# Second token tile routed first and its table rows requested earlier; one-hot rows laid out slot, token, key, with gate parts on ScalarE

## The chip, the cores and the metric

The kernel runs on one core of one Trainium2 chip. The metric is device microseconds of one execution. Three timed runs of the kernel before gave a median of 1670.44 us (1669.8 to 1672.08). The profiled execution took 1673.91 us; its span, from the first to the last instruction that the profile shows, is 1672.1 us.

## The reference

Two transformer blocks in sequence over 256 tokens of width 1024. The part that the change touches is the PEER layer at the end of the first block, which lets each token pick 128 of 16,384 small experts and sums their outputs:

```python
def peer(h, w_pq, sub_keys, u_emb, v_emb):
    q = (h @ w_pq).reshape(B, S, 8, 2, 128)
    sc = jnp.einsum("bshcd,hcnd->bshcn", q, sub_keys)      # 8 heads x 2 halves x 128 keys
    s_top, i_top = lax.top_k(sc, 16)
    cand = s_top[..., 0, :, None] + s_top[..., 1, None, :]
    cand_idx = i_top[..., 0, :, None] * 128 + i_top[..., 1, None, :]
    best, pos = lax.top_k(cand.reshape(B, S, 8, 256), 16)
    expert_idx = jnp.take_along_axis(cand_idx.reshape(B, S, 8, 256), pos, axis=-1)
    gate = jax.nn.softmax(best, axis=-1)
    # per token c, experts e: 8 heads x 16
    a = jax.nn.gelu(jnp.einsum("ced,cd->ce", u_emb[idx], hx), approximate=False)
    return jnp.einsum("ce,ced->cd", g * a, v_emb[idx])
```

`u_emb` and `v_emb` are tables of 16,384 rows of 1024 floats, 64 MB each.

## The kernel before, in words

Nearly all weights stream from HBM in blocks of 128x1024 floats (512 KB), issued by SyncE. A weight block of the ordinary layers is split into a high part (`whi`, made on ScalarE) and a low part (`wlo` = raw - high, made on VectorE, or on GpSimd for the blocks whose number is in `POOL`), and 24 matmuls use it (lines 145 to 147).

The PEER layer runs as follows (function `peer`). In this text a *u-block* is one block of 128 rows of the table u, a *v-block* the same of v.

1. Query stage. 16 weight blocks of `w_peer_q` (numbers 66 to 81) give the queries; `scores(h, c, qt)` makes the scores of head h, half c for the two token tiles `tt` = 0 and 1 (tokens 0 to 127 and 128 to 255). VectorE starts the routing from them: `unit(tt, h, ...)` finds the top 16 of both halves and of their sums, `select(tt, h0)` turns positions into expert numbers for four heads (`isel`, `jsel`), `gates()` makes the softmax (`ex`) and the expert number (`ei`). These are Python generators in the list `bg`; `pump(budget)` takes steps from its head until the budget, in microseconds of VectorE, is used. Where the instructions finally stand on an engine is set by a list scheduler with its own costs, not by the order of the calls alone.
2. u stage. 128 u-blocks (`ublock`), each 16 matmul instructions (line 976) and a Gelu into the array `G`. They serve tokens 0 to 159 densely (N = 160): all 16,384 experts are computed. The transfer of a block is asked for when one of ten buffers of the ring comes free.
3. One-hots. For four tokens at a time (40 groups), `onehots` makes Q and O, which compare `jT` and `iT` with the row of numbers `io`, and P and R, which are O times the high and the low part of the gate; `place` multiplies Q with P and R on TensorE (line 1009, 8 matmuls), and the result multiplies `G` (line 1015 on VectorE). So gates are spread over the dense grid of experts.
4. Rows. Tokens 160 to 255 are not computed densely: for them GpSimd asks for single table rows with an indirect DMA, 128 rows of 4 KB (512 KB) in one instruction (line 1555). There are two row groups, 192 to 255 and 160 to 191, together 96 row transfers of u, then 96 of v, into six buffers. A u transfer is followed by a dot product on VectorE (`dot`, line 1560), a v transfer by a multiply-add (`axpy`, line 1570). `some_rows(rate)` after each block takes steps of this sequence; the first row needs `idx`, which `indices` makes from `ei` by matmuls with `spread` (line 1547) and a copy on VectorE (line 1550).
5. v stage. 128 v-blocks, each 16 matmul instructions (line 1064), with the rest of the rows beside them, then the sum and the next layer.

Before the change `gates()` is called once for both token tiles, behind 46 u-blocks (`I0`); its transposes and index matmuls stand behind u-block 47 on TensorE.

Of the kernel before, what the change touches and what calls it, by code (L numbers as in the profile page):

```python
# [20 lines left out]
T = 256  # L21
# [38 lines left out]
POOL = range(4, 52)  # L60
# [11 lines left out]
QP = 1.3  # L72
UP = 2.0

NT = 4
RG = 0
# [9 lines left out]
class Kernel:  # L86
# [710 lines left out]
    def peer(self):  # L797
# [6 lines left out]
        iT = p2h.tile([128, T], F16, name="iT")  # L804
        jT = p2h.tile([128, T], F16, name="jT")
# [3 lines left out]
        gTl = p2h.tile([128, T], F16, name="gTl")  # L809
# [44 lines left out]
        def select(tt, h0):  # L854
# [40 lines left out]
        scs = {}  # L895

        def scores(h, c, qt):
            for tt in range(2):
# [24 lines left out]
        def gates():  # L923
            nc.vector.scalar_tensor_tensor(ei, isel, float(N_KEYS), jsel, op0=ALU.mult, op1=ALU.add)
            nc.vector.tensor_tensor(ex, best, best[:, :, :, 0:1].to_broadcast([128, 2, 8, 16]), op=ALU.subtract)
            nc.scalar.activation(ex, ex, AF.Exp)
            sm = p2t.tile([128, 2, 8], F32, name="sm", bufs=1)
            nc.vector.reduce_sum(sm, ex, axis=AX.X)
            nc.vector.reciprocal(sm, sm)
            nc.vector.tensor_mul(ex, ex, sm[:, :, :, None].to_broadcast([128, 2, 8, 16]))  # L930
# [11 lines left out]
            self.later(1, turn)  # L942

# [43 lines left out]
        def onehots(t0, oh, io):  # L987

            ts = slice(t0, t0 + NT)
            Q, O, P, R = (oh.tile([128, 128, NT], F16, name=n, bufs=2) for n in ("Q", "O", "P", "R"))  # L990
            col = lambda v: v[:, None, ts].to_broadcast([128, 128, NT])
            nc.vector.tensor_tensor(Q, io, col(jT), op=ALU.is_equal)
            nc.vector.tensor_tensor(O, io, col(iT), op=ALU.is_equal)
            nc.vector.tensor_mul(P, O, col(gTh))
            if t0 >= RG:
                for k in range(NT):
                    nc.scalar.activation(R[:, :, k], O[:, :, k], AF.Copy, scale=gT[:, t0 + k:t0 + k + 1])
            else:
                nc.vector.tensor_mul(R, O, col(gTl))
            return Q, (P, R)  # L1000

        def place(t0, n_i, oh):

            pt = self.pp.tile([128, 4, 128], F32, name="ax", bufs=4)
            Q, Ps = oh
# [16 lines left out]
        for i in range(I0):  # L1022
            ublock(i, 0)
            self.pump(UP if i < I0 - 2 else 1e9)
# [753 lines left out]
```

## Time and profile before

| | |
|---|---|
| timed runs, median (range) | 1670.44 us (1669.8 to 1672.08) |
| profiled execution / its span | 1673.91 us / 1672.1 us |
| TensorE busy over the span | 1594.9 us (95%) |
| VectorE / ScalarE / GpSimd busy | 68% / 38% / 21% |
| chain that ended last, over the span | PE 60%, DMA 19%, DVE 17% |
| u stage / v stage, from the timeline | 339.4 to 705.9 us / 705.9 to 1013.4 us |

In the profile PE is TensorE, PEld its weight loads, DVE VectorE, ACT ScalarE, POOL GpSimd, SP SyncE, which issues the block transfers. A group of instructions is named by its line, its engine, its operation and output<-input tiles; "idle before" is the time for which the engine stood still just ahead of them, with what ended it. In the tables of stretches, the DMA share is the mean busy share of the core's 16 DMA engines and GB/s what they moved.

### The profile page before, as it was taken

Reading aid. Unit: us, or ns where it says so; the run is one execution under the profiler, and the core shown is the slowest. Engines: PE = TensorE matmul, PEld = TensorE weight load, DVE = VectorE, ACT = ScalarE, POOL = GpSimd, SP = SyncE. Lnnn points to the kernel's source line nnn. Section 1 sums busy time; section 2 is a strip of 40 time slices with the busy share of each in tenths; the row PEclk is TensorE's granted clock in tenths of the full one; section 3 lists DMA queues with packets and bytes.
Section 4 is the critical chain, followed back from the end, with each engine's and each line's share of the span. In section 5 each row is a group of like instructions: output and inputs, shape, how many; then the busy total and the mean of one; then the engine's idle time right before and its main releaser. Section 6 shows DMA issues by size and latency. Waiting matters only on the chain.

```text
span 1672.1 us, 29794 instructions
## 1 busy us (share of the span) xinstructions
PE 1594.9 (95%) x11502; PEld 1504.6 (90%) x11502; DVE 1142.8 (68%) x2599; ACT 637.1 (38%) x1373; POOL 347.1 (21%) x288
## 2 busy tenths in 40 slices
PE   8989989998989899899999999999999999999998
PEld 7878979998989899899888999887999998799986
DVE  7989978898178899854544007866776557676654
ACT  4557545531233343200000005455544445555443
POOL 3734630000045454543332000100000020000000
PEclk9989989999999999899999999999999999999999
DMA  5522437576799999999999865732755677365563
GB/s 184 171 80 93 137 123 228 160 252 198 239 402 406 408 381 409 395 409 409 409 409 409 317 196 159 246 102 87 224 185 182 186 189 211 94 188 183 180 189 113
DMA packets 109388, 398.97 MB, mean 239 GB/s; under 512 B 12484, under 2 KB 12643, under 8 KB 108736
## 3 DMA queue, kind: packets, MB, share of 16 engines
q1 hardware_dynamic: 78336, 282.63, 50.0%
q0 software_dynamic: 30768, 114.39, 18.1%
q8 instruction: 90, 1.47, 0.4%
q14 instruction: 50, 0.41, 0.1%
q10 hardware_dynamic: 144, 0.07, 0.0%
HBM read 394.86 MB, written 6.11 MB: 240 GB/s over the span
## 4 chain that ended last, share of the span: by engine, by line
PE 60%; DMA 19%; DVE 17%; issue 3%; ACT 1%; POOL 1%; SPq 0%; DVEq 0%; POOLq 0%; ACTq 0%
PE mm L145 12%; PE mm L146 11%; PE mm L147 11%; PE ax L1064 9%; DMA row<-un,idx 8%; DMA raw<-vv 4%; DMA whi<-vv 4%; PE mm L976 3%; DVE junk L1560 2%; DVE ax L589 2%; PE mm L213 1%; DVE wlo L126 1%; PE mm L211 1%; PE mm L212 1%; PE ax L442 1%
## 5 line engine op out<-in xcount | busy, mean ns | idle before, releaser
L122 ACT ACTIVATE whi<-raw 128x1024 fp32r<-128x1024 f32 x275 | 290.3, 1058 | 620.1 <-DMA raw<-wst 310.0
L126 DVE TENSOR_TENSOR wlo<-raw,whi 128x1024 fp32r<-128x1024 f32 x227 | 277.3, 1223 | 187.8 <-ACT whi L122 184.3
L145 PE MATMUL mm<-xgh,whi 128*128 128x256 f32 x1064 | 304.3, 286 | 0.0
L147 PE MATMUL mm<-xgh,wlo 128*128 128x256 f32 x1064 | 301.8, 284 | 0.4 <-DVE wlo L126 0.4
L146 PE MATMUL mm<-xgl,whi 128*128 128x256 f32 x1064 | 301.4, 283 | 0.0
L145 PEld LDWEIGHTS mm<-xgh,whi 128*128 128x128 f32 x1064 | 201.9, 190 | 1.1 <-issue 0.8
L147 PEld LDWEIGHTS mm<-xgh,wlo 128*128 128x128 f32 x1064 | 201.9, 190 | 0.7 <-DVE wlo L126 0.6
L146 PEld LDWEIGHTS mm<-xgl,whi 128*128 128x128 f32 x1064 | 202.0, 190 | 0.1
L1570 DVE SCALAR_TENSOR_TENSOR acc<-row,w,acc 128x1024 f32<-128x1024 f32 x94 | 120.7, 1284 | 111.1 <-DMA row<-vv,idx 111.0
L1555 POOL DMA_INDIRECT row<-un,idx x96 | 105.5, 1099 | 277.6 <-DVE idx L1550 169.4
L1560 DVE CUSTOM_DVE_ANT_0 junk<-row,h 128x1024 f32<-128x1024 f32 x96 | 117.5, 1224 | 33.9 <-DMA row<-un,idx 32.4
L124 POOL TENSOR_TENSOR wlo<-raw,whi 128x1024 fp32r<-128x1024 f32 x48 | 115.1, 2403 | 107.8 <-ACT whi L122 105.0
L1064 PE MATMUL ax<-G,raw 128*128 128x160 f32 x832 | 125.6, 303 | 3.1 <-DMA raw<-vv 1.0
L1555 POOL DMA_INDIRECT row<-vv,idx x96 | 96.7, 1008 | 142.8 <-DVE acc L1570 123.5
L1064 PEld LDWEIGHTS ax<-G,raw 128*128 128x128 f32 x832 | 116.1, 191 | 8.1 <-DMA raw<-vv 7.7
L976 PE MATMUL mm<-hn,raw 128*128 128x160 f32 x816 | 121.6, 304 | 0.1
L976 PEld LDWEIGHTS mm<-hn,raw 128*128 128x128 f32 x816 | 116.5, 195 | 0.4 <-ACT G L984 0.3
L146 PE MATMUL mm<-hl,whi 128*128 128x256 f32 x368 | 106.8, 290 | 2.2 <-DVE hl L356 2.1
L976 PE MATMUL mm<-hn,wlo 128*128 128x160 f32 x608 | 95.3, 313 | 5.0 <-ACT G L979 5.0
L589 DVE SCALAR_TENSOR_TENSOR ax<-u,cw,ax 128x256 f32<-128x256 f32 x227 | 97.7, 481 | 0.7
L1064 PE MATMUL ax<-G,wlo 128*128 128x160 f32 x608 | 93.6, 306 | 2.2 <-DMA wlo<-vv 0.6
L976 PEld LDWEIGHTS mm<-hn,wlo 128*128 128x128 f32 x608 | 90.5, 201 | 5.2 <-ACT G L979 5.2
(435 smaller groups left out, 3358.2 us busy)
## 6 DMA issues: line engine op xcount, KB each, us to landing
raw<-wst SPq DMA_DIRECT2D x278, 512.0 KB, 3.7
raw<-vv SPq DMA_DIRECT2D x52, 512.0 KB, 15.1
raw<-ut SPq DMA_DIRECT2D x51, 512.0 KB, 6.6
whi<-ut SPq DMA_DIRECT2D x39, 512.0 KB, 6.6
wlo<-ut SPq DMA_DIRECT2D x38, 512.0 KB, 6.7
wlo<-vv SPq DMA_DIRECT2D x38, 512.0 KB, 14.9
whi<-vv SPq DMA_DIRECT2D x38, 512.0 KB, 15.5
tabr<-tabd POOLq DMA_DIRECT2D x1, 2048.0 KB, 8.3
```

Of the source, the lines that this page charges most:

```text
L122: nc.scalar.activation(hi, raw, AF.Copy)
L124: nc.gpsimd.tensor_sub(lo, raw, hi)
L126: self.pin = nc.vector.tensor_sub(lo, raw, hi)
L145: nc.tensor.matmul(pt, w[:, s], xs[0][:, k], start=first, stop=False)
L146: nc.tensor.matmul(pt, w[:, s], xs[1][:, k], start=False, stop=False)
L147: nc.tensor.matmul(pt, lo[:, s], xs[0][:, k], start=False, stop=last)
L589: nc.vector.scalar_tensor_tensor(y[:, c] if k == 30 else ps, u[:, c, k:k + T], cw[:, c, k:k + 1], ps, op0=ALU.mult, op1=ALU.add)
L976: nc.tensor.matmul(pt, raw[:, k * 128:(k + 1) * 128], hn[:, k, :N], start=(k == 0), stop=(k == C - 1))
L1064: nc.tensor.matmul(acc[d // 2][:, d % 2, :N], raw[:, d * 128:(d + 1) * 128], G(i), start=False, stop=False, skip_group_check=True)
L1555: self.k.nc.gpsimd.indirect_dma_start(t, None, table, bass.IndirectOffsetOnAxis(ap=self.idx[:, s:s + 1], axis=0))
L1560: self.k.nc.vector.tensor_tensor_reduce(junk, row, self.h, 1.0, 0.0, ALU.mult, ALU.add, self.a[:, s:s + 1])
L1570: self.k.nc.vector.scalar_tensor_tensor(self.acc, row, w, self.acc, op0=ALU.mult, op1=ALU.add)
```

## The change

Routing order: `scores` handles token tile 1 first and puts the routing of tile 1 ahead of tile 0 in `bg`; `gates(tt)` is one call for each tile, and the one of tile 1 also starts the row requests (`indices`). The 16 query blocks get their `wlo` on GpSimd, and the budgets are new (QP from 1.3 to 2.8; UP from 2.0 to 2.1 and, once the rows are asked for, 1.4). For tile 0 one of the three wide operations of `select` runs on GpSimd. The u-blocks run without a fixed I0 until `bg` is empty, with `some_rows(0.68)` after each once the rows are asked for, and `some_rows(0.8)` after each v-block; before, both rates were 197 steps over 206 blocks.

One-hots: Q and O become one tile QO (slot, token, key) from one VectorE instruction with three buffers; P and R are both made on ScalarE by 8 scaled copies of 128 elements, where R alone took 4.

```diff
-POOL = range(4, 52)
+POOL = (*range(4, 52), *range(66, 82))
-QP = 1.3
-UP = 2.0
+QP = 2.8
+UP = (2.1, 1.4)
+RU = 0.68
+RV = 0.8
...
-                nc.vector.tensor_mul(e4, e4, tops[:, tt, c, h0:h0 + nh, None, :].to_broadcast([128, nh, 16, 16]))
+                eng.tensor_tensor(e4, e4, tops[:, tt, c, h0:h0 + nh, None, :].to_broadcast([128, nh, 16, 16]), op=ALU.mult)
...
-            for tt in range(2):
+            for tt in (1, 0):
...
-                self.bg.append(turns(*(unit(tt, h, [scs[tt, h, i] for i in range(2)]) for tt in range(2))))
-                if h % 4 == 3:
-                    self.bg.extend([select(tt, h - 3) for tt in range(2)])
+                u0, u1 = (unit(tt, h, [scs[tt, h, i] for i in range(2)]) for tt in range(2))
+                firsts.append(u1)
+                self.bg.insert(next((k for k, u in enumerate(self.bg) if k and u not in firsts), len(self.bg)), u1)
+                self.bg.append(u0)
...
             def turn():
-                for n, src in enumerate((isel, jsel, ex)):
-                    pt = self.pp.tile([128, T], F32, name="ax", bufs=4)
-                    for tt in range(2):
-                        nc.tensor.transpose(pt[:, tt * 128:(tt + 1) * 128], src[:, tt].rearrange("p a b -> p (a b)"), self.ident)
-                    nc.scalar.activation((iT, jT, gT)[n], pt, AF.Copy, scale=(1.0, 1.0, G_SCALE)[n])
-                self.split(gT, gTh, gT)
-                nc.scalar.activation(gTl, gT, AF.Copy)
-                for g in rows:
-                    g.indices()
+                if tt == 1:
+                    for g in rows:
+                        g.indices()
+                    asked.append(tt)
+                pt = self.pp.tile([128, 3, 128], F32, name="ax", bufs=4)
+                for n, src in enumerate((jsel, isel, ex)):
+                    nc.tensor.transpose(pt[:, n], at(src).rearrange("p a b -> p (a b)"), self.ident)
+                nc.scalar.activation(jiT[:, :, ts], pt[:, :2], AF.Copy)
+                nc.scalar.activation(gT[:, ts], pt[:, 2], AF.Copy, scale=G_SCALE)
+                self.split(gT[:, ts], gTh[:, ts], gTl[:, ts])
             self.later(1, turn)
...
-            Q, O, P, R = (oh.tile([128, 128, NT], F16, name=n, bufs=2) for n in ("Q", "O", "P", "R"))
-            col = lambda v: v[:, None, ts].to_broadcast([128, 128, NT])
-            nc.vector.tensor_tensor(Q, io, col(jT), op=ALU.is_equal)
-            nc.vector.tensor_tensor(O, io, col(iT), op=ALU.is_equal)
-            nc.vector.tensor_mul(P, O, col(gTh))
...
+            QO = oh.tile([128, 2, NT, 128], F16, name="QO", bufs=3)
+            P, R = (oh.tile([128, NT, 128], F16, name=n, bufs=2) for n in ("P", "R"))
+            nc.vector.tensor_tensor(QO, io[:, None, None, :].to_broadcast([128, 2, NT, 128]),
+                                    jiT[:, :, ts, None].to_broadcast([128, 2, NT, 128]), op=ALU.is_equal)
+            for k in range(NT):
+                for dst, g in ((P, gT), (R, gTl)):
+                    nc.scalar.activation(dst[:, k], QO[:, 1, k], AF.Copy, scale=g[:, t0 + k:t0 + k + 1])
...
-        I0 = 46
-        for i in range(I0):
+        k = next((k for k, u in enumerate(self.bg) if k and u not in firsts), len(self.bg))
+        self.bg[k:k] = [select(1, 0, nc.vector), select(1, 4, nc.vector), gates(1)]
+        self.bg += [select(0, 0, nc.gpsimd), select(0, 4, nc.gpsimd), gates(0)]
+        done, i = 0, 0
+        while self.bg:
             ublock(i, 0)
-            self.pump(UP if i < I0 - 2 else 1e9)
-        gates()
-        done, i = 0, I0
+            self.pump(UP[len(asked)])
+            if asked:
+                some_rows(RU)
+            i += 1
```

Three places show how instructions move. The first is TensorE in the u stage before the change: the matmuls on `hn` are u-blocks (x8 is one block; the profile shows each of its matmuls as two instructions), and 47 blocks stand ahead of the transposes of `isel`, `jsel`, `ex` and the index matmuls on `spread`.

```order
L976 MATMUL mm<-hn,raw 128x160 x8
L976 MATMUL mm<-hn,whi 128x160 x8
L976 MATMUL mm<-hn,wlo 128x160 x8
L936 MATMUL ax<-ident,isel 128x128 x2
L936 MATMUL ax<-ident,jsel 128x128 x2
L936 MATMUL ax<-ident,ex 128x128 x2
L1547 MATMUL ax<-ei,spread_4060 128x128
L1547 MATMUL ax<-ex,spread_4060 128x128
```

After the change the index matmuls of tile 1 stand behind u-block 11; this is TensorE there.

```order
L987 MATMUL mm<-hn,raw 128x160 x16
L1560 MATMUL ax<-ei,spread_4209 128x128
L1560 MATMUL ax<-ex,spread_4209 128x128
L1560 MATMUL ax<-ei,spread_4219 128x128
L1560 MATMUL ax<-ex,spread_4219 128x128
L948 MATMUL ax<-ident,jsel 128x128
L948 MATMUL ax<-ident,isel 128x128
L948 MATMUL ax<-ident,ex 128x128
```

The transposes of tile 0 follow behind u-block 36, and the first one-hot product stands behind u-block 40 (before: behind block 49). The second place is VectorE just ahead of the first one-hots, before the change: no dot product (`junk<-row`) precedes the first Q.

```order
L1550 CAST idx_4064<-ax 32x32
L1551 COPY gate_4065<-ax 32x32
L1035 CAST io<-iota 128x512
L1067 MEMSET zeros 128x512
L992 TENSOR_TENSOR Q<-io,jT 128x512
L993 TENSOR_TENSOR O<-io,iT 128x512
L994 TENSOR_TENSOR P<-O,gTh 128x512
L1560 ISA junk,a_4056<-row,h_4052 128x1024
```

The same place after the change.

```order
L1573 ISA junk,a_4205<-row,h_4201 128x1024
L1573 ISA a_4205 128x1
L358 TENSOR_TENSOR gTl<-gT,gTh 128x128
L1049 CAST io<-iota 128x128
L1080 MEMSET zeros 128x512
L1003 TENSOR_TENSOR QO<-io,jiT 128x1024 x3
L1573 ISA junk,a_4205<-row,h_4201 128x1024
```

30 dot products stand ahead of the first QO, between it and the copies to `idx`; before the last QO of the 40 there are 140 row steps (96 dots, 44 multiply-adds), where before the change 100 stood ahead of the last Q (96 and 4). The third place is GpSimd. Before, its row transfers follow the `park` transfer, with nothing between them:

```order
L124 TENSOR_TENSOR wlo<-raw,whi 128x1024 x48
L811 DMA sk<-subk 128x2048
L802 DMA park<-x 128x2048
L1555 DMA row<-un,idx_4054 128x1024 x64
L1555 DMA row<-un,idx_4064 128x1024 x32
```

The same place after the change:

```order
L813 DMA sk<-subk 128x2048
L126 TENSOR_TENSOR wlo<-raw,whi 128x1024 x2
L804 DMA park<-x 128x2048
L126 TENSOR_TENSOR wlo<-raw,whi 128x1024 x14
L1568 DMA row<-un,idx_4203 128x1024 x11
L885 TENSOR_TENSOR eq<-eq,tops 128x1024
L1568 DMA row<-un,idx_4203 128x1024 x2
```

GpSimd has 16 more low parts ahead of the row transfers, and the four products of `select` for tile 0 stand among the first 18 of them, the first behind 11.

## Rows read from the trace of the kernel before

**Rows 1.** Stretches: us, busy (instructions) of PE, PEld, DVE, ACT, POOL; clock, DMA, GB/s.

```profile
276.00:339.00 63.00, 62.86 (x535) 62.51 (x533) 55.30 (x230) 32.97 (x70) 0.55 (x1) 1.00 0.60 195
339.00:390.00 51.00, 51.00 (x382) 50.90 (x382) 51.00 (x287) 13.53 (x31) 0.00 (x0) 1.00 0.73 237
390.00:396.00 6.00, 1.23 (x10) 0.98 (x8) 5.96 (x43) 1.84 (x3) 0.00 (x0) 0.81 0.56 190
...
480.00:520.00 40.00, 33.30 (x249) 32.55 (x248) 31.30 (x70) 14.07 (x58) 18.84 (x18) 1.00 1.03 407
...
456.00:706.00 250.00, 224.89 (x1611) 220.78 (x1610) 212.81 (x481) 91.34 (x368) 124.14 (x111) 0.96 1.01 397
706.00:925.00 219.00, 211.43 (x1438) 198.93 (x1437) 108.86 (x88) 0.00 (x0) 78.73 (x82) 0.99 1.03 409
```

**Rows 2.** Timeline of TensorE, u-blocks and index matmuls: start, length, line, tiles, count.

```profile
428.85 2.34 PE L976 MATMUL mm<-hn,raw 128*128 128x160 f32 x16
...
450.59 2.34 PE L976 MATMUL mm<-hn,raw 128*128 128x160 f32 x16
...
453.42 0.39 PE L1547 MATMUL ax<-ei,spread 128*128 128x128 f32 x2
```

**Rows 3.** Timeline of VectorE: routing from its start to the expert numbers.

```profile
294.16 2.85 DVE L891 SCALAR_TENSOR_TENSOR hn<-x,prm,rb 128x256 f32<-128x256 f32 x7
...
385.80 0.29 DVE L818 MAX8 tv<-sc 128x8 f32<-128x128 f32 x1
...
393.27 0.19 DVE L861 TENSOR_SCALAR q<-pos 128x64 uint32<-128x64 uint32 x1
...
411.77 0.43 DVE L924 SCALAR_TENSOR_TENSOR ei<-isel,jsel 128x256 f32<-128x256 f32 x1
```

**Rows 4.** Block transfers of table u issued by 456 us: ns, first to last start.

```profile
L966 SPq DMA_DIRECT2D raw<-ut x23: 327/328/328, 320.8 to 453.0; - x23
L966 SPq DMA_DIRECT2D whi<-ut x17: 327/328/423, 332.5 to 448.6; - x17
L966 SPq DMA_DIRECT2D wlo<-ut x17: 327/328/902, 333.0 to 450.8; - x17
```

**Rows 5.** DMA issues, 456 to 706 us: count, KB, median us to landing.

```profile
raw<-vv SPq DMA_DIRECT2D x4, 512.0 KB, 7.9
row<-un,idx POOLq DMA_INDIRECT x96, 11.1
wlo<-vv SPq DMA_DIRECT2D x3, 512.0 KB, 7.8
whi<-vv SPq DMA_DIRECT2D x3, 512.0 KB, 7.6
row<-vv,idx POOLq DMA_INDIRECT x15, 11.4
```

**Rows 6.** DMA issues, 706 to 925 us.

```profile
row<-vv,idx POOLq DMA_INDIRECT x81, 13.7
```

**Rows 7.** Chain that ended last, in order of time, through the v stage.

```profile
705.92 72.19 PE ax L1064 x512
778.13 20.67 DMA raw<-vv
...
923.13 75.52 PE ax L1064 x554
```

**Rows 8.** Groups by line, VectorE, 456 to 706 us: busy, mean ns, idle before.

```profile
L1560 DVE CUSTOM_DVE_ANT_0 junk<-row,h 128x1024 f32<-128x1024 f32 x96 | 117.5, 1224 | 33.9 <-DMA row<-un,idx 32.4 <-DVE O L993 0.5
L992 DVE TENSOR_TENSOR Q<-io,jT 128x512 f16<-128x512 f16 x40 | 16.8, 420 | 0.0
```

**Rows 9.** Groups by line and shape, VectorE, 339 to 412 us.

```profile
L879 DVE TENSOR_TENSOR eq<-f,iota 128x1024 f32<-128x1024 f32 x8 | 9.8, 1220 | 0.0
```

**Rows 10.** Groups by line, ScalarE, 456 to 706 us.

```profile
L997 ACT ACTIVATE R<-O,gT 128x128 f16<-128x128 f16 x160 | 63.0, 585 | 1.8 <-DVE O L993 1.8
```

**Rows 11.** Line 124, low parts on GpSimd: duration ns min/median/max, first to last.

```profile
L124 POOL TENSOR_TENSOR wlo<-raw,whi x48: 2337/2397/2607, 22.4 to 230.0; 128x1024 fp32r<-128x1024 f32 x48
```

More of the change, by code (lines that the diff above doesn't have):

```diff
@@ L803, in peer @@
         hn = p2h.tile([128, C, T], F32, name="hn")
-        iT = p2h.tile([128, T], F16, name="iT")
-        jT = p2h.tile([128, T], F16, name="jT")
+        jiT = p2h.tile([128, 2, T], F16, name="jiT")
         gT = p2h.tile([128, T], F32, name="gT")
         gTh = p2h.tile([128, T], F16, name="gTh")
-        gTl = p2h.tile([128, T], F16, name="gTl")
+        gTl = p2h.tile([128, T], F32, name="gTl")
         sk = p2q.tile([128, 16, 128], F32, name="sk")
@@ L852, in unit, with select @@
             yield from top16(best[:, tt, h], pos[:, tt, h], cd, w)
-        def select(tt, h0):
+        def select(tt, h0, eng):
             nh = 4
@@ L895, in peer @@
         scs = {}
+        firsts = []
         def scores(h, c, qt):
-            for tt in range(2):
+            for tt in (1, 0):
                 sp = self.pp.tile([128, 128], F32, name="ax", bufs=4)
@@ L921, in peer, with gates @@
         ex = p2t.tile([128, 2, 8, 16], F32, name="ex")
[L923 to L928, printed above, removed]
+        asked = []
+        def gates(tt):
+            at = lambda t: t[:, tt]
+            nc.vector.scalar_tensor_tensor(at(ei), at(isel), float(N_KEYS), at(jsel), op0=ALU.mult, op1=ALU.add)
+            nc.vector.tensor_tensor(at(ex), at(best), best[:, tt, :, 0:1].to_broadcast([128, 8, 16]), op=ALU.subtract)
+            nc.scalar.activation(at(ex), at(ex), AF.Exp)
+            sm = p2t.tile([128, 8], F32, name="sm", bufs=1)
+            nc.vector.reduce_sum(sm, at(ex), axis=AX.X)
@@ L942, in gates @@
             self.later(1, turn)
+            yield 1.5
         self.close("p2q")
@@ L989, in onehots @@
             ts = slice(t0, t0 + NT)
-            Q, O, P, R = (oh.tile([128, 128, NT], F16, name=n, bufs=2) for n in ("Q", "O", "P", "R"))
-            col = lambda v: v[:, None, ts].to_broadcast([128, 128, NT])
-            nc.vector.tensor_tensor(Q, io, col(jT), op=ALU.is_equal)
-            nc.vector.tensor_tensor(O, io, col(iT), op=ALU.is_equal)
-            nc.vector.tensor_mul(P, O, col(gTh))
[L995 to L1000, printed above, removed]
+            QO = oh.tile([128, 2, NT, 128], F16, name="QO", bufs=3)
[5 more added lines that the diff above has]
+                    nc.scalar.activation(dst[:, k], QO[:, 1, k], AF.Copy, scale=g[:, t0 + k:t0 + k + 1])
+            return QO, (P, R)
         def place(t0, n_i, oh):
             pt = self.pp.tile([128, 4, 128], F32, name="ax", bufs=4)
-            Q, Ps = oh
+            QO, Ps = oh
             for t in range(4):
@@ L1008, in place @@
                     k = (t0 + t) % NT
-                    nc.tensor.matmul(pt[:, t], Q[:, :, k], P[:, :, k], start=P is Ps[0], stop=P is Ps[-1])
+                    nc.tensor.matmul(pt[:, t], QO[:, 0, k], P[:, k], start=P is Ps[0], stop=P is Ps[-1])
             for k in range(2):
@@ L1033, in peer @@
         poh = self.open("poh", side="left")
-        io = poh.tile([128, 128, NT], F16, name="io")
-        nc.vector.tensor_copy(io, self.iota[:, :, None].to_broadcast([128, 128, NT]))
+        io = poh.tile([128, 128], F16, name="io")
+        nc.vector.tensor_copy(io, self.iota)
         i0 = i
         n_g = N // 4
-        rate = fetch_steps() / (254.0 - i0)
         for g in range(n_g):
@@ L1043, in peer @@
                 ublock(i, 4 * done)
-                some_rows(rate)
+                some_rows(RU)
                 i += 1
@@ L1049, in peer @@
             ublock(i, N)
-            some_rows(rate)
+            some_rows(RU)
             i += 1
@@ L1075, in peer @@
                 vmm(blk, d)
-            some_rows(rate)
+            some_rows(RV)
         self.close("pgb")
@@ L1088, in peer @@
                 vmm(blk, d)
-            some_rows(rate)
+            some_rows(RV)
         for _ in fetch:
@@ L1574, in add @@
         self.k.nc.tensor.matmul(o[:, self.t0:self.t0 + self.n], self.acc[:, c * 128:(c + 1) * 128], self.fold, start=False, stop=last, skip_group_check=True)
-def fetch_steps():
-    return 2 * sum(n for _, n in ROWS) + RB - 1
 def fetched(groups):
```

7 lines of the change are left out of this document (4 added, 3 removed).

## The prediction

> **What bounds the kernel now.** I read the table of stretches first, then the chain, then the timelines and DMA issues of the stretches that the change touches. In the stretches [rows 1] the reader is to see four states of the PEER layer. In the query stage (276 to 339 us) TensorE is full. From 339 to 390 us TensorE and VectorE are both full and the DMA engines move 237 GB/s: a u-block takes TensorE (450.59 - 428.85) / 10 = 2.174 us [rows 2], and 512 KB (0.524 MB) in that time is 241 GB/s. From 456 to 706 us, with the row transfers running, the DMA engines move 397 GB/s, and 409 from 706 to 925 us; TensorE has gaps there. So the DMA engines are the limit from the first row request until the rows are through, and TensorE before and after. Then the chain [rows 7]: TensorE runs unhindered from 705.92 to 778 us on blocks that were fetched ahead, then steps of some 20 us that end on v-blocks alternate with nothing else until 923 us, then TensorE alone, to the end of the stage at about 1013.4 us.
>
> Before 456 us some 409 - 241 = 168 GB/s lie idle. That is because the index matmuls stand behind u-block 47 and start only at 453.42 us [rows 2], though the expert numbers are finished at 411.77 + 0.43 = 412.2 us [rows 3].
>
> **When the first row is asked for after the change (T0).** On VectorE, from its start at about 293.4 us (294.16 less part of the low part ahead of it) to the copies to `idx`, the order shows the scaling of `hn` (8 x 0.4 = 3.3 us), 14 units (8 of tile 1, 6 of tile 0), two selects, gates for one tile and some set-up. Two units take 393.27 - 385.80 = 7.47 us, so 14 take 52.3. From 393.27 to 411.77 us VectorE does two selects and the gates of both tiles: 18.5 us, less about 0.7 for the smaller gates. Sum 3.3 + 52.3 + 17.8 + 2 for set-up and copies = 75.4, so 369 us. Before, the steps of both tiles alternated; now many wait for their predecessor, for which I add 0 to 8 us and take 4: T0 = 373 us. The scores are no limit: the last ones stand ahead of the u stage at 339 us, when half of this work is left. TensorE reaches the index matmuls behind block 11 at 339.4 + 11 x 2.174 = 363 us and waits little; `ei` is ready 3 units (11 us) ahead of the copies. The wait costs 0 to 5 us of TensorE, which it has to spare (below).
>
> **The u stage, by DMA transfers.** Count 512 KB transfers. By 456 us, 23 + 17 + 17 = 57 blocks were issued [rows 4]: the 47 that TensorE had done and the ring of ten. From 456 to 706 us 71 u-blocks, 4 + 3 + 3 = 10 v-blocks and 96 + 15 = 111 rows followed [rows 5]: 192 transfers in 250 us, 0.768 a us.
>
> At T0 after the change TensorE has done (373 - 339.4) / 2.174 = 15.5 blocks, with the ring 26 issued. At the end of the u stage 138 are issued as before. The rows by then are set by VectorE's order: TensorE can't finish the one-hot products before VectorE has made the last QO, and 140 row steps stand ahead of that, where 100 stood before. Before, 111 were issued when the stage ended, 11 more than the order asks; the same now gives 151. So 138 - 26 + 151 = 263 transfers, at 0.768 a us 342 us: the stage ends at 373 + 342 = 715 us, 9 us later than the 706 before, with 40 more rows fetched. If those 11 shrink to 6, it ends at 709; I take 713. Per us of T0, only (0.768 - 0.46) / 0.768 = 0.4 us is lost, since u-blocks flow meanwhile at 1 / 2.174 = 0.46.
>
> What must fit under it. TensorE: 128 x 2.174 = 278 us, 320 one-hot matmuls, and stalls: from 390 to 396 us [rows 1] it waited for ScalarE, which sat behind the Exp of the gates. Now there are two Exps; the second, behind the Gelu of block 24, waits for VectorE and may cost 7 to 10 us. With at most 0.14 us for each one-hot matmul, TensorE would be through at 339 + 278 + 45 + 15 = 677 us, 36 ahead. It will wait at block 40 (its 30 dots come ahead of the first QO: 50 blocks and some 36 rows, 60 transfers after T0, 78 us, 451 us), but this is the same DMA time again. VectorE: 212.81 us busy in the stage before [rows 1] for 107 row steps and 40 groups. From 451 us on it has 116 row steps (+9 x 1.22 = 11 us [rows 8]), 37 QO instead of 120 instructions of 0.42 us (-50), and 9 more blocks (+2). At 1.22 us for a QO it is 221 us of 263, 84% as before (85%). ScalarE: 8 copies a group at 0.585 us [rows 10] is 4.7 us of a group time of 7: hidden, and if not, a copy that is late holds the product of its group. GpSimd in the query stage: 2.40 us a low part [rows 11] against 24 x 63 / 535 = 2.83 us of TensorE a block [rows 1]: hidden; without that cover each of 16 would cost up to 2.4 us.
>
> The QO instruction itself isn't in the trace. Bounds: 0.42 us x 2 = 0.84 us for 1024 elements by the two-byte row for 512 [rows 8], 1.22 us by the four-byte row for 1024 [rows 9]. I take 1.22, the dearer, since one operand now stands still along the inner dimension. The Trainium skill ("VectorE: DVE Perf Modes", "What auto-detection actually checks") says that two results a cycle need every tensor 16-bit with step 1 or -1; the operand `jiT` has step 0, so that rule speaks against the change: three fast instructions become a slow one. By the rule the 37 QO take 45 us, without it 31; neither moves the sum, as the DMA engines end last by 40 us.
>
> **The v stage.** Before, 705.9 to 1013.4: 307.5 us with its tail. Its matmuls run at 75.52 / 554 = 0.1363 us when nothing is missing [rows 7], so the 1438 from 706 to 925 us [rows 1] need 196 of 219 us: 23 us lost to the DMA engines, all after the unhindered 72 us, so 23 / 147 = 0.16 us a us. The rows came at 81 in 203 us (706 to 909), 0.40 a us [rows 6]. After the change 192 - 151 = 41 to 46 are left, gone after 103 to 115 us; past the first 72 that is 31 to 43 us at 0.16, 5 to 7 us lost instead of 23. So the stage takes 307.5 - 17 = 290.5 us, bounds 284.5 (nothing lost) and 300.
>
> **Sum.** 713 + 290.5 = 1003.5 against 1013.4, so -10 us. Made against the profiled execution (1673.91 us, of which 1672.1 are span and the 1.8 around it stay) this gives 1664; that execution is 3.5 us over the median of the runs, which goes from 1670.44 to 1660. What lies ahead and behind is unchanged. The change buys little because the u stage is as full as before and only takes over rows that the v stage paid for.
>
> **Rivals.**
> *Better overlap* (bigger gain): with a third QO buffer and P off VectorE, the DMA engines run at the 409 GB/s of the next stretch, 0.78 transfers a us; T0 is 369 (24 blocks issued) and 146 rows come by the end: 138 - 24 + 146 = 260 transfers, 333 us, the u stage ends at 702, and the v stage loses nothing (284.5): 987, -27, 1643. For it: TensorE was idle for 250 - 224.89 = 25 us of this stage [rows 1]. Against: the DMA engines moved 397 GB/s through those gaps.
> *Rows hidden anyway* (no change): VectorE's interleaved routing delays the dots, and with them the freeing of six row buffers, so that T0 is 380 (0.4 x 7 = 3 us) and the rate until 451 us some 0.69 instead of 0.768 (71 x 0.08 = 5.5 transfers, 7 us). The gain of 10 is gone. For it: while the rows run, dots are spread between routing steps; against: six buffers hide some of that. Time 1670.
> *VectorE's queue as the bound* (slower): 30 dots stand ahead of the first QO and three a group after it, each waiting for its row in order, with QO, the products into `G` and so TensorE behind them. It decides once VectorE's busy share in the stage falls under 221 / (263 + 10) = 81%. In the first 40 us of full DMA load before, 480 to 520, it was 31.30 / 40 = 78% [rows 1]; at that share 221 us take 283, the stage ends at 451 + 283 = 734 and the v stage (289) at 1023: +9, 1680. For it: 32.4 us of waits of dots for rows before [rows 8]; against: three QO buffers.
>
> **Chances.** Forecast 0.53, better overlap 0.22, no change 0.13, slower 0.12. A difference under 0.2% (3.3 us) can't be told from none. The forecast's own spread is 1652 to 1668 (5 us from the count of rows, 4 from T0 and stalls each way); of the better case 1644 and up is taken in, of the slower one only what ends by 1671, so about 0.18 is left out. Faster 0.76, same 0.12, slower 0.12: the better case and nine tenths of the forecast are faster, and the unchanged case has its edges on both sides.
>
> **What would show it.** The first row request at 368 to 380 us; first one-hot product at 445 to 460 us; DMA engines full from about 375 us; end of the u stage within 705 to 722 us; rows through at 810 to 835 us instead of 909, and TensorE alone at 2.18 us a v-block afterwards; QO at about 1.2 us. The prediction is wrong if the DMA engines stay under 390 GB/s between 451 and 700 us (then VectorE bounds), if TensorE loses time in the query stage, or if far fewer than 140 rows are in by the end of the u stage.

## The result, and the profile after

The changed kernel takes 1699.63 us (median of 4 runs, 1696.7 to 1700.08) against 1670.12 us of the kernel before in the same session (1669.34 to 1672.08): 1.0171 times as long, interval 1.0154 to 1.0189. Slower by 1.7%, clear of the noise, where 1660 us was forecast. The profiled execution took 1699.78 us, with a span of 1698.0.

The stretches after, with the columns of [rows 1]: the query stage, the u stage up to the first row request, up to the first one-hot product, to its end, and two parts of the v stage.

```profile
276.00:345.00 69.00, 66.18 (x548) 65.63 (x548) 62.91 (x217) 34.72 (x77) 39.09 (x17) 0.98 0.57 189
345.00:394.00 49.00, 37.99 (x272) 37.65 (x271) 48.93 (x266) 13.24 (x28) 0.27 (x1) 0.90 0.48 159
394.00:480.00 86.00, 58.07 (x413) 57.47 (x411) 65.64 (x162) 10.29 (x29) 49.84 (x40) 0.85 0.98 373
480.00:755.00 275.00, 235.03 (x1734) 222.02 (x1735) 233.51 (x384) 133.02 (x550) 160.99 (x120) 0.95 1.01 399
755.00:925.00 170.00, 169.29 (x1226) 167.76 (x1226) 52.43 (x43) 0.00 (x0) 36.72 (x37) 0.99 0.93 354
925.00:1042.00 117.00, 117.00 (x873) 117.00 (x871) 6.32 (x13) 6.66 (x15) 0.00 (x0) 1.00 0.64 208
```

Two things stand against [rows 1]. From the first u-block to the first one-hot product (345 to 480 us) TensorE idles 39 us; [rows 1] shows one gap of 5 there. And the u stage ends at 754.7 us instead of 705.7. The v stage that follows is shorter, 286.7 us instead of 307.1, with TensorE almost never idle; it gives back 20 of the 49 us.

VectorE in the query stage (276 to 345 us, groups by line and shape: busy, mean ns, idle before):

```profile
L893 DVE SCALAR_TENSOR_TENSOR hn<-x,prm,rb 128x256 f32<-128x256 f32 x8 | 9.4, 1250 | 1.2 <-ACT rb L353 1.2
L387 DVE SCALAR_TENSOR_TENSOR xgl<-x,prm,xgh 128x256 fp32r<-128x256 f32 x5 | 7.9, 1581 | 2.1 <-ACT xgh L386 2.1
L843 DVE CAST tops<-iu 128x16 f32<-128x16 uint32 x13 | 5.1, 389 | 0.1
L850 DVE TENSOR_TENSOR cd<-tv 128x48 f32<-128x48 f32 x6 | 4.6, 762 | 0.0
L850 DVE TENSOR_TENSOR cd<-tv 128x64 f32<-128x64 f32 x6 | 4.4, 730 | 0.0
L820 DVE MAX8 tv<-sc 128x8 f32<-128x128 f32 x14 | 3.8, 281 | 0.0
L385 DVE TENSOR_TENSOR x<-mm,xt 128x256 f32<-128x256 f32 x4 | 1.7, 418 | 0.0
```

Of the kernel before, the same groups in its query stage (276 to 345 us) show what these instructions cost without low parts on GpSimd:

```profile
L891 DVE SCALAR_TENSOR_TENSOR hn<-x,prm,rb 128x256 f32<-128x256 f32 x8 | 3.3, 478 | 0.0
L841 DVE CAST tops<-iu 128x16 f32<-128x16 uint32 x16 | 2.5, 164 | 0.0
L385 DVE SCALAR_TENSOR_TENSOR xgl<-x,prm,xgh 128x256 fp32r<-128x256 f32 x5 | 2.4, 479 | 0.0
L848 DVE TENSOR_TENSOR cd<-tv 128x48 f32<-128x48 f32 x8 | 1.7, 207 | 0.0
L848 DVE TENSOR_TENSOR cd<-tv 128x64 f32<-128x64 f32 x8 | 1.8, 223 | 0.0
L818 DVE MAX8 tv<-sc 128x8 f32<-128x128 f32 x16 | 4.1, 283 | 0.0
L383 DVE TENSOR_TENSOR x<-mm,xt 128x256 f32<-128x256 f32 x4 | 1.7, 423 | 0.0
```

The instructions are the same. These with two inputs in SBUF (`hn`, `xgl`, `cd`) last 2.6 to 3.7 times as long, and the cast 2.4 times, while MAX8 (one input) and the addition with an input from PSUM (`mm`) are as before. Not every instruction with two SBUF inputs is longer: `sq<-sq,sqq` has them too and stays at 416 ns (418 before), since none of its four began while a low part ran.

The longest waits of TensorE and ScalarE (engine, line, what it waited for: us in total, times, longest), TensorE from 340 to 1042 us, ScalarE from 340 to 480:

```profile
PE ax L1017 <- ACT P L1007: 25.0, 6, 15.8
PE mm L987 <- ACT G L990: 23.7, 2, 12.7
...
ACT ex L934 <- DVE ex L933: 33.9, 2, 17.8
```

The 23.7 us are the two Exps: ScalarE stands in front of each, waiting for its input, with the Gelus queued behind it. The 15.8 us end at the first one-hot product, at 480.7 us.

### The profile page after: what moved, and what is told of

Read it like the earlier page. It is cut to its first block, busy times and chain, and to the rows that moved or that the text cites. A ratio compares the mean times of both kernels' runs of the same rounds, so it can differ in the third digit from the quotient of the medians.

```text
span 1698.0 us, 29932 instructions
## 1 busy us (share of the span) xinstructions
PE 1577.1 (93%) x11502; PEld 1488.8 (88%) x11502; DVE 1155.1 (68%) x2510; ACT 678.3 (40%) x1549; POOL 430.4 (25%) x308
## 4 chain that ended last, share of the span: by engine, by line
PE 60%; DVE 18%; DMA 14%; issue 4%; POOL 2%; ACT 1%; SPq 0%; DVEq 0%; POOLq 0%; ACTq 0%
PE ax L1077 14%; PE mm L147 11%; PE mm L148 11%; PE mm L149 11%; DMA row<-un,idx 6%; DMA row<-vv,idx 4%; PE mm L987 2%; DVE ax L591 2%; PE mm L215 1%; PE mm L213 1%; PE ax L444 1%; PE mm L214 1%; DVE junk L1573 1%; DVE acc L1583 1%; DMA wlo<-vv 1%
## 5 line engine op out<-in xcount | busy, mean ns | idle before, releaser
L128 DVE TENSOR_TENSOR wlo<-raw,whi 128x1024 fp32r<-128x1024 f32 x211 | 257.9, 1224 | 277.9 <-ACT whi L124 271.6
L126 POOL TENSOR_TENSOR wlo<-raw,whi 128x1024 fp32r<-128x1024 f32 x64 | 153.5, 2403 | 138.1 <-ACT whi L124 135.3
L1568 POOL DMA_INDIRECT row<-un,idx x96 | 113.7, 1185 | 148.7 <-PE mm L987 57.0
L1568 POOL DMA_INDIRECT row<-vv,idx x96 | 121.6, 1266 | 107.1 <-DVE acc L1583 61.2
L987 PE MATMUL mm<-hn,raw 128*128 128x160 f32 x816 | 125.5, 311 | 3.4 <-ACT G L995 3.1
L987 PE MATMUL mm<-hn,whi 128*128 128x160 f32 x624 | 96.4, 310 | 16.0 <-ACT G L990 11.0
L987 PEld LDWEIGHTS mm<-hn,whi 128*128 128x128 f32 x624 | 90.2, 197 | 22.9 <-ACT G L990 11.3
L987 PE MATMUL mm<-hn,wlo 128*128 128x160 f32 x608 | 93.7, 309 | 15.8 <-ACT G L990 12.7
```

The lines of the kernel that those rows point to most:

```text
L126: nc.gpsimd.tensor_sub(lo, raw, hi)
L128: self.pin = nc.vector.tensor_sub(lo, raw, hi)
L987: nc.tensor.matmul(pt, raw[:, k * 128:(k + 1) * 128], hn[:, k, :N], start=(k == 0), stop=(k == C - 1))
L1568: self.k.nc.gpsimd.indirect_dma_start(t, None, table, bass.IndirectOffsetOnAxis(ap=self.idx[:, s:s + 1], axis=0))
```

## The experiments

All times below are medians of 4 runs (e3: 10) beside the kernel before on the same chip, 1669.06 to 1671.31 us. Positions are from the traces, in us; "u stage ends" is the start of the first v product, and rows are those issued by then.

| kernel | first row asked for | first one-hot product | u stage ends | last v product | rows | time | ratio to before (95%) |
|---|---|---|---|---|---|---|---|
| before | 456.1 | 459.1 | 705.7 | 1012.8 | 111 | 1670.12 | |
| after | 393.7 | 480.7 | 754.7 | 1041.4 | 156 | 1699.63 | 1.0154 to 1.0189 |
| e1 before, low parts on GpSimd | 470.9 | 473.8 | 721.5 | 1029.0 | 111 | 1685.87 | 1.0072 to 1.0111 |
| e2 after, low parts on VectorE | 378.6 | 461.8 | 735.6 | 1022.8 | 153 | 1683.05 | 1.0058 to 1.0104 |
| e3 before, new one-hots | 456.7 | 459.6 | 701.7 | 1010.1 | 106 | 1668.09 | 0.9976 to 0.9996 |
| e4 after, row steps pinned | 393.2 | 463.6 | 675.9 | 998.2 | 80 | 1655.19 | 0.9882 to 0.9927 |
| e5 = e4 + e2 | 379.7 | 453.1 | 665.4 | 987.3 | 80 | 1644.61 | 0.9829 to 0.9870 |
| e6 = e5, Exps later | 380.3 | 444.5 | 656.8 | 976.2 | 80 | 1635.93 | 0.9782 to 0.9823 |
| e7 = e6, 0.85 steps a block | 381.3 | 452.0 | 664.2 | 973.9 | 100 | 1632.23 | 0.9752 to 0.9798 |
| e8 before, row steps pinned | 455.5 | 458.4 | 668.6 | 996.6 | 76 | 1655.67 | 0.9901 to 0.9941 |
| e9 = e7, row gates read behind Exp | 376.7 | 451.9 | 659.9 | 969.9 | 100 | 1630.37 | 0.9738 to 0.9770 |
| e10 = e9, 1.0 steps a block | 378.4 | 465.2 | 680.8 | 989.8 | 117 | 1648.57 | 0.9841 to 0.9874 |
| e11 = e8 + e3 | 456.0 | 458.9 | 651.9 | 987.1 | 76 | 1646.59 | 0.9831 to 0.9865 |
| e12 = e11, 1.25 times the steps | 456.2 | 459.1 | 682.4 | 995.0 | 94 | 1653.58 | 0.9884 to 0.9933 |

In e6 and e7 the rows' gates are read ahead of the Exps, so the rows are weighted without the softmax; the instructions are the same in number and size.

**e1 and e2: the low parts on GpSimd, alone and taken away.**

```diff
# e1, in the kernel before
-POOL = range(4, 52)
+POOL = (*range(4, 52), *range(66, 82))
# e2, in the changed kernel
-POOL = (*range(4, 52), *range(66, 82))
+POOL = range(4, 52)
```

> The kernel before with one edit: the low parts of the 16 query blocks move from VectorE to GpSimd. Theory (GpSimd holds up those VectorE instructions that read two SBUF tiles): hn takes about 1.25 us each instead of 0.48, the last xgl 1.6 to 3 us instead of 0.48, cd 0.75 us instead of 0.22; the first u-block starts near 344 us instead of 339.4. The Exp of the gates now stands behind the Gelu of block 10, its input comes near 390 us, so TensorE loses 15 us or more there: 1680 to 1692 us. Rival (GpSimd only takes work off VectorE): the routing ends 16 us earlier, u-block 1 stays at 339 us, 1665 to 1672 us.

> The changed kernel with one edit: the 16 query low parts go back to VectorE. Theory of the shared access: u-block 1 back at 339.5 us, hn at 0.48 us, first row request 388 us or earlier although VectorE has 18 us of low parts more; 5 to 14 us faster than the changed kernel, 1685 to 1695 us, still slower than before because 137 row steps stay ahead of the last QO. Rival (the contention is only a symptom, VectorE's load decides): first row request at 405 us or later, 1700 us or more.

Lines of e1 (276 to 420 us), then of e2, by group:

```profile
L891 DVE SCALAR_TENSOR_TENSOR hn<-x,prm,rb 128x256 f32<-128x256 f32 x8 | 9.5, 1253 | 1.2 <-ACT rb L351 1.2
```

```profile
L893 DVE SCALAR_TENSOR_TENSOR hn<-x,prm,rb 128x256 f32<-128x256 f32 x8 | 3.3, 478 | 0.0
```

That one line of the change makes the kernel before 16 us slower, and without it the changed kernel is 16.6 us faster; `hn` follows it both times. In e1 the first u-block starts at 343.4 us instead of 339.6, and TensorE then waits 16.1 us for the Exp instead of 5.0: together the 15 us by which the first row is late. The gain of e2 is larger than the 5 to 14 us that I expected, though its first u-block starts at 342.2 us and not at 339.5. The line is half of the loss and a little more: e2 is still 13 us slower than before.

**e3: the one-hots alone.** The kernel before with QO, P and R as after, and their products.

```diff
-            Q, O, P, R = (oh.tile([128, 128, NT], F16, name=n, bufs=2) for n in ("Q", "O", "P", "R"))
+            QO = oh.tile([128, 2, NT, 128], F16, name="QO", bufs=3)
...
-                    nc.tensor.matmul(pt[:, t], Q[:, :, k], P[:, :, k], start=P is Ps[0], stop=P is Ps[-1])
+                    nc.tensor.matmul(pt[:, t], QO[:, 0, k], P[:, k], start=P is Ps[0], stop=P is Ps[-1])
```

> The kernel before with the new one-hots alone (QO in one VectorE instruction, P and R on ScalarE). Theory (the one-hots are not where the time went): QO 1.22 us against three instructions of 0.42, ScalarE 8 x 0.40 against 4 x 0.585 us a group, DMA engines still full: within 4 us of before, 1666 to 1674 us. Rival (the longer chain VectorE, ScalarE, TensorE is what made the change slow): 1680 us or more.

Within 0.24% of before, so the one-hots are not the cause. Their products last 219 ns instead of 296 (QO and P now lie contiguous in key), which at this point TensorE can't use.

**e4: the row steps pinned.** Dots and multiply-adds that are due in the one-hot part may be issued on VectorE only behind the product into `G` of the latest u-block (`gm`), so that the scheduler can't draw them ahead. 69 row steps stand ahead of the last QO, instead of 140.

```diff
+            with self.tc.issue_after(gm[0].ins) if gm[0] is not None else nullcontext():
-            while owed >= 1.0:
+                while owed >= 1.0:
...
-                nc.vector.tensor_mul(G(i, slice(0, n_t)), G(i, slice(0, n_t)), ac[:, :n_t])
+                gm[0] = nc.vector.tensor_mul(G(i, slice(0, n_t)), G(i, slice(0, n_t)), ac[:, :n_t])
```

> The changed kernel with the row steps of the one-hot part of the u stage held behind VectorE's product of the u-block at which they are called, so 0.68 a block: 69 row steps instead of 140 stand ahead of the last QO, 15 instead of 30 ahead of the first. Theory (the loss is in rows carried by the u stage, which waits for them, while the v stage can give back only what it lost to the DMA engines): u stage ends at 680 to 705 us instead of 755, v stage grows to 305 to 315 us from 287, in all 1645 to 1675 us. Rival (the loss is in the early stalls at the Exps and in the contention): 1690 us or more.

Stretches of e4, in the columns of [rows 1]:

```profile
464.00:560.00 96.00, 96.00 (x788) 95.32 (x786) 70.02 (x136) 67.27 (x259) 24.55 (x26) 1.00 0.96 352
560.00:676.00 116.00, 116.00 (x943) 115.02 (x943) 90.60 (x178) 67.76 (x273) 33.12 (x33) 1.00 0.98 369
676.00:760.00 84.00, 84.00 (x619) 83.83 (x618) 42.13 (x58) 0.23 (x1) 34.42 (x36) 1.00 1.03 408
760.00:880.00 120.00, 113.02 (x744) 101.92 (x742) 59.96 (x47) 0.00 (x0) 43.40 (x46) 1.00 1.03 409
```

From the first one-hot product to 760 us TensorE is never idle, at 352 and 369 GB/s in place of 399. Against after, the u stage carries 76 rows less and ends 78.8 us earlier, 1.04 us a row; the v stage is 322.3 us instead of 286.7, 0.47 us a row more. So these 76 rows cost, on average, twice as much in the u stage as in the v stage. The kernel is 44 us faster for nothing but the place of these instructions on VectorE.

**e5: both.** e4 with the edit of e2.

> The changed kernel with its row steps pinned behind the u-blocks' products, as in the paced run before (1655.19), and with the low parts of the query chunks 66 to 81 on VectorE again instead of GpSimd. My theory: the two losses are separate, the rows that the u stage carries (taken away by the pins) and VectorE's instructions that GpSimd's low parts hold up. hn is back at 478 ns and xgl at 479, the first Exp of the gates is no longer waited for (the unpinned kernel without the low parts on GpSimd had one stall of 10.4 us in place of two), the first row is asked for near 378 us instead of 393.2, the first one-hot product near 450 instead of 463.6, and since TensorE is never idle from there to the end of the u stage in the paced run, this comes out at the end whole: 1655 - 13 = 1642, 1636 to 1648. Rival (DMA is what ends the kernel even with the pins, so that an earlier start of the one-hot part gives nothing): the v stage gets longer by as much as the u stage ends earlier, 1652 to 1657. Rival 2 (the two losses were one and the same): also 1652 to 1657, with hn still near 1250.

As the first theory says: the first product, the end of the u stage and the last v product all come 10.5 to 11 us earlier than in e4. One wait for an Exp is left, as expected (10.3 us of TensorE).

**e6 and e7: the Exps later, then more row steps.**

```diff
# e6: Exp, sums and normalising move from gates() into turn(), behind the latest Gelu (ge)
-            nc.scalar.activation(at(ex), at(ex), AF.Exp)
...
             def turn():
+                with self.tc.issue_after(ge[0].ins):
+                    nc.scalar.activation(at(ex), at(ex), AF.Exp)
# e7
-RU = 0.68
+RU = 0.85
```

> The kernel of the run with pins and without the low parts on GpSimd, in which each of the two Exps of the gates is put on ScalarE behind the Gelu of one of the latest u-blocks (behind Gelu 11 and 35 instead of 5 and 25). My theory: TensorE's waits of some 10 us each in the u stage are ScalarE standing in front of an Exp whose operand VectorE has not made yet, with the Gelus that free TensorE's mm buffers queued behind it. One such stall was left without the low parts on GpSimd (10.4 us), so the kernel is faster by 6 to 11 us than the one with pins and without those low parts: near 1633 if that one comes out at 1642. Rival (VectorE's work on the selection and the gates sets the start of the one-hot part, and TensorE waits for it somewhere in any case): the wait of 10 us moves to before the first one-hot product, the first product stays at the same time, and the u-blocks done before it are the same in number, so no difference, within 3 us.

> As the run with the pinned Exps, but with 0.85 instead of 0.68 row steps for each u-block: 87 row steps ahead of the last one-hot rows instead of 69. My theory says that a row step in the u stage costs only where DMA or VectorE's queue ahead of the one-hots becomes the bound: the paced run moved 352 to 369 GB/s in that stage where 409 is the most that any stage showed, and VectorE was busy 76%, so some 18 more rows (some 23 us of transfer at 0.768 a us) fit nearly in its 212 us, and the v stage, which ran at 409 GB/s with TensorE idle some 15 us of 322, loses that idle time: 5 to 12 us faster than with 0.68. Rival (each row step ahead of a one-hot costs TensorE its 2.4 us on VectorE, at any rate): 18 steps x some 2.5 us = up to 40 us longer u stage, 15 to 30 us slower at the end.

TensorE's waits in e6, 340 to 1010 us; the group `PE mm <- ACT G` is gone:

```profile
PE ax L952 <- DVE ex L949: 3.5, 1, 3.5
PE ax L1086 <- DMA raw<-vv: 2.7, 4, 1.4
PE ax L1086 <- DMA whi<-vv: 1.4, 1, 1.4
```

e6 is 8.7 us faster than e5, of the 10.3: the stall came from the place of the Exp in ScalarE's queue, not from VectorE's work. e7 is another 3.7 us faster, less than the 5 to 12 expected, and the intervals of the two overlap. The v stage is 9.7 us shorter (309.7 instead of 319.4; I expected some 15), but the first product comes 7.5 us later, with 20 dots ahead of the first QO instead of 15. From the first product to the end of the u stage both take 212 us: the 15 rows that come on top there cost nothing.

**e8, e11 and e12: what is the early routing worth?** The pins in the kernel before (the edit of e4), then with the one-hots of e3, then with more steps.

```diff
# e12
-        rate = fetch_steps() / (254.0 - i0)
+        rate = 1.25 * fetch_steps() / (254.0 - i0)
```

> The kernel before with nothing but the pins: its row steps wait for the product of a u-block already written, as in the paced run of the changed kernel (65 row steps ahead of the last one-hot rows instead of 100). This tells how much of the paced run's gain is the early routing. My theory: with the rows asked for only at 456 us, DMA has some 395 transfers left (81 blocks of ut, 128 of vv, 192 rows less the few issued), 515 us at 0.768 a us, so that it ends at 970 whatever the pins do, and the 40 us of work behind it stay; u stage ends at 680 to 695 instead of 706, v stage takes the difference on, and the kernel is at 1660 to 1672, within 0.6% of before (1670). Rival (pacing alone is the whole gain, early routing is worth nothing): as the paced run of the changed kernel or better, 1645 to 1656.

> The kernel before with the pins (1655.67 alone) and the new one-hots, so all of the paced run without low parts on GpSimd (1644.61) but the early routing. My theory: the new one-hots take VectorE time from the u stage, which TensorE bounds once the rows are pinned, and so give only what their shorter products give TensorE (320 x 0.08 us, most of it beside other matmuls): 1650 to 1656, and the early routing is worth the other 6 to 11 us. Rival (the early routing is worth nothing, the new one-hots are): 1643 to 1648.

> The kernel before with the pins and the new one-hots (1646.59), and a quarter more row steps for each u-block (81 ahead of the last one-hot rows instead of 63). This is to tell what the early routing is worth when the rest is as good: the best kernel with it, 0.85 steps and 87 ahead of the last one-hot rows, is at 1630.37. My theory: without it the rows start at 456 us, DMA then moves 387 and 408 GB/s of 409 in the u stage already, so 18 more rows (23 us of transfer) find room for 6 us only; the u stage ends 15 us later (667 instead of 652) and the v stage gives back the 19 us that TensorE idles in it, at most: 1641 to 1648, no difference of weight, and the early routing with its freed DMA time is worth some 10 to 15 us. Rival (the early routing is worth nothing, the number of steps is all): 1629 to 1635.

My theory for e8 fell: at 1655.67 it is as fast as the paced changed kernel. The last row was asked for at 965.3 us, near the 970 at which I had the transfers end, but 31 us of work came behind it and not 40. So of the 44 us that the pins bring the changed kernel, 13 are to be had in the kernel before too (1669.06 to 1655.67). And the paced changed kernel had lost about as much to the low parts on GpSimd (10.6 us, e5) as its one-hots bring (9.1 us, e11). My theory for e11 fell too: with TensorE as the bound the shorter products do pay, and the u stage ends 16.7 us earlier than in e8; half of it is left at the end. So all of e5's gain is had without early routing: e5 makes 0.68 steps a block and has 80 rows in the u stage, e11 makes 197 / 206 = 0.96 and has 76 (1644.61 and 1646.59 us). With more rows in the u stage it is not. e12's u stage, in the columns of [rows 1]:

```profile
456.00:560.00 104.00, 98.56 (x789) 96.51 (x788) 85.13 (x164) 67.55 (x264) 50.58 (x42) 0.98 1.00 394
560.00:663.00 103.00, 94.37 (x749) 91.30 (x745) 95.67 (x181) 59.66 (x241) 59.21 (x43) 0.98 1.03 408
```

Here the DMA engines are full from the first row on (394 and 408 GB/s) and 18 more rows make the u stage 30 us longer, twice what I expected; the kernel is 7 us slower than e11, where I had no difference. e7 put 20 more in for 7 us. The difference of e12 and e9, 1653.58 and 1630.37, holds the early routing and the later Exps. The latter were 8.7 us in e6, and e12's own wait for the Exp is 5.0 us, so by estimate 15 to 18 us are left for the earlier start of the rows. No run separates the two here.

**e9 and e10: the best version, and a step too far.** e9 is e7 with the rows' gates read behind the Exps and the gates' transposes two u-blocks later; e10 has `RU = 1.0`.

```diff
+                if tt == 1:
+                    for g in rows:
+                        g.gates()
                 pt = self.pp.tile([128, 3, 128], F32, name="ax", bufs=4)
```

> As the run with the pinned Exps and 0.85 row steps for each u-block (1632.23), with the rows' gates read behind the Exps (the two runs with pinned Exps read them ahead, so that their rows were weighted without the softmax), and the gates' transposes two u-blocks later. My theory: the Exps and the gates behind them set no time once they stand late enough, so the only wait of TensorE left between the first u-block and the first one-hot product, 7.8 us before the transposes, goes too: 1624 to 1632. Rival (VectorE's selection of the tokens ahead of it is what the transposes wait for, and the wait moves with them): 1631 to 1635.

> The same with 1.0 row steps for each u-block (104 ahead of the last one-hot rows, 87 before). My theory: with 0.85, DMA moved 389 and 404 GB/s in the two halves of the one-hot part, of 409 at most, and TensorE was busy all the time; 17 more rows, 22 us of transfer, have no room there. The u stage gets 10 to 20 us longer and the v stage, in which TensorE waits 8 us for DMA, can give back no more than that: 3 to 12 us slower than with 0.85. Rival (the steps are free as long as they are paced): the v stage gains its 8 us and the u stage is as long, 4 to 8 us faster.

TensorE's longest waits, 340 to 1010 us, of e9 and of e10:

```profile
PE ax L1577 <- DVE ex L949: 7.8, 1, 7.8
PE ax L955 <- DVE ex L949: 1.6, 1, 1.6
```

```profile
PE ax L955 <- DVE ex L949: 9.1, 1, 9.1
PE ax L1577 <- DVE ex L949: 9.1, 1, 9.1
PE ax L1094 <- ACT G L1037: 4.5, 1, 4.5
```

e9, with nothing left out, takes 0.9754 of the time before (0.9738 to 0.9770) and is 69 us faster than the changed kernel. Its wait did not go; 7.8 us long as in e7, it moved from the transposes to the gates' index matmuls, as the rival said, and 1630.37 against e7's 1632.23 is no difference that these runs show. e10 is 18.2 us slower than e9, more than expected: 13 us of it are there before the first product. The dots due before it are not pinned, and stand between the steps of the gates on VectorE (27 ahead of the first QO, 22 in e9).

## Why the prediction was wrong, point by point

**The step that failed first** is "GpSimd in the query stage: 2.40 us a low part against 2.83 us of TensorE a block: hidden". The low parts were as long as forecast (2403 ns) and TensorE did not wait for them; VectorE did, and through VectorE TensorE too (2.6 us for `xgl`, the first u-block at 344.4 us instead of 339.6). I priced the cover on the engine that uses the result, not on the one that GpSimd holds up. The trace of before shows it a stage earlier, where GpSimd made low parts already. VectorE at 114 to 125 us (start, length), where `qT` has two inputs in SBUF and `q<-ax,st` one in PSUM:

```profile
114.92 0.42 DVE L651 TENSOR_TENSOR q<-ax,st 128x256 f32<-128x256 f32 x1 [0.79 <-PE ax L649]
115.26 0.41 DVE L652 TENSOR_TENSOR q<-q,ct 128x256 f32<-128x256 f32 x1
...
116.05 2.57 DVE L653 TENSOR_TENSOR qT<-q,q 128x256 f32<-128x256 f32 x1
...
123.47 2.20 DVE L653 TENSOR_TENSOR qT<-q,q 128x256 f32<-128x256 f32 x1
```

and GpSimd:

```profile
115.98 2.35 POOL L124 TENSOR_TENSOR wlo<-raw,whi 128x1024 fp32r<-128x1024 f32 x1 [7.15 <-ACT whi L122]
122.93 2.47 POOL L124 TENSOR_TENSOR wlo<-raw,whi 128x1024 fp32r<-128x1024 f32 x1 [4.60 <-ACT whi L122]
```

Both `qT` end 0.3 us after GpSimd's operation (118.62 against 118.33, 125.67 against 125.40): they stood still until it was over. Their mean of 1166 ns beside 422 for the other form would have told it.

The change brings the same a second time: the four products of `select` on GpSimd, ahead of the first one-hot product. Two of them in the changed kernel, and what VectorE did beside them:

```profile
431.62 2.63 POOL L885 TENSOR_TENSOR eq<-eq,tops 128x1024 f32<-128x1024 f32 x1
431.99 2.35 DVE L877 TENSOR_TENSOR f<-f 128x64 f32<-128x64 f32 x1
438.17 1.17 DVE L1573 CUSTOM_DVE_ANT_0 junk<-row,h 128x1024 f32<-128x1024 f32 x1
438.28 3.27 POOL L885 TENSOR_TENSOR eq<-eq,tops 128x1024 f32<-128x1024 f32 x1 [1.38 <-DVE sm L937]
```

The same `f` took 222 ns in the kernel before. Two of the four `f` and a cast stand still for 2.1 us each in this way, and VectorE once waits 2.2 us for the product: 8.6 us for the 4.9 us of products that GpSimd took over. e9 still has it (an `f` of 2.37 and one of 3.04 us). No run takes these products back, so their share of the time stays open.

**T0 = 373 us**: 393.7. Against the forecast's working, `hn` is done 11.2 us later (298.44 + 9.45 against 293.4 + 3.3; it begins 5.0 us late), 12 `cd` cost 6.4 us more and 13 `tops` 2.9 us: 20.5 of 20.7. e2 gives 15.1 of it back, although VectorE makes the 16 low parts itself there.

**The end of the u stage, 713 us**: 754.7, which is 41.7 late. 20.7 are T0. By T0 24 blocks were issued, not 26, and 156 rows by the end, not some 149: 9 transfers more, 11.7 us at 0.768 a us. The 270 transfers went at 0.748 a us, which is the other 9.3 us; from 394 to 480 us the engines moved 373 GB/s. The count of 140 row steps from VectorE's order, and the rule that the stage lasts as long as its transfers, were right.

**The stalls.** Two Exps cost 23.7 us of TensorE; I priced the second alone, at 7 to 10, in 15 us for all stalls. "36 ahead" was to cover them, but both stand ahead of the first product, as the slower routing does, and that came at 480.7 us instead of 451.

**What the sum took as given** is that the rows in the u stage are a fixed count set by VectorE's order. They are, but the count need not be what it is. The forecast had the prices: 1 / 0.768 = 1.3 us for a row in the u stage, and 17 us for 40 rows, 0.4 each, in the v stage. It did not draw from them that 40 more rows in the u stage are a loss by themselves; e4 measures 1.04 and 0.47. The forecast's TensorE bound, 677 us, is where e4's u stage ends (675.9) once 80 rows stand in it instead of 156, but this is in part luck: e4's first u-block comes at 343.9 us instead of 339 and its stalls are 22.8 us instead of 15, so that only 31 us are left for the one-hot products and the rest, where the forecast had 45.

**The rival "VectorE's queue as the bound"** named the mechanism (dots ahead of the one-hots, TensorE behind them) and gave 1680 us. Its point of decision was wrong: VectorE was busy 85% from 480 to 755 us, above the 81% below which it was to decide. VectorE's queue and the DMA engines are one chain there: dots waited 25.1 us for their rows in this stretch.

**Right**: the v stage (290.5, measured 286.7), the traffic while one-hots and rows run (399 GB/s from 480 us, 397 before), the QO at 1.22 us, and ScalarE's copies hidden (0.40 us each):

```profile
L1003 DVE TENSOR_TENSOR QO<-io,jiT 128x1024 f16<-128x1024 f16 x40 | 48.7, 1222 | 0.0
L1007 ACT ACTIVATE P<-QO,gT 128x128 f16<-128x128 f16 x160 | 63.9, 399 | 22.2 <-DVE QO L1003 21.9
```

## What to carry to other kernels

Before work moves to GpSimd, look in the trace for VectorE instructions of the neighbourhood with two SBUF inputs, and at their longest beside their shortest: the cost falls on them, not only on the engine that waits for the result. Where optional work (row fetches, their dots) shares an in-order queue with what TensorE needs, count what stands ahead in that queue and pin it; a rate in the source says nothing once a scheduler draws work forward. A gain that starts transfers earlier is worth something only when the stage that then takes them has room.

## What the hardware showed that I had not expected

While GpSimd runs a `TENSOR_TENSOR` from SBUF, a VectorE instruction with two SBUF inputs waits for its end: on average 479 to 1581 ns (`xgl`), 478 to 1250 (`hn`), and the cast 164 to 389. The low parts lose nothing by it (median 2397 ns before and after). But it goes the other way too: the four `eq` products took 2.64, 3.39, 2.63 and 3.27 us, where the shortest of e2 took 2.37. Each began while a dot (two SBUF inputs) ran on VectorE, and is longer by about what was left of that dot: 0.35, 1.15, 0.37 and 0.99 us were left. The Trainium skill ("SBUF — State Buffer", "Who interferes with whom") states this: an instruction with two SBUF inputs contends with a GpSimd instruction that reads SBUF, and so does a cast that runs in a two-port mode; whichever issues first has the shared ports and the other fully blocks, while a VectorE instruction with at most one SBUF input, outside the two-port modes, does not contend. The trace agrees, MAX8 and the addition from PSUM included (283 and 281, 423 and 418 ns). One record does not fit: an `xgl` that begins 0.30 us ahead of a low part (288.30 and 288.60 us) still ends 0.29 us behind it.

A matmul of 128x128 two-byte values lasts 219 ns with contiguous operands (e3), and 296 ns where neighbouring keys lie four elements apart (before; medians, both operands changed together).
